# Encoder layer on one core: a factor spread at once over all partitions with its by-token values sent through DRAM, transposes issued in one row, a second norm in four steps, and final results multiplied from PSUM

## The chip, the cores and the metric

The kernel runs on 1 core of one Trainium2 chip. The metric is the device time of one execution in microseconds (us); the time of a kernel is the median of its runs. Engines are named as in the profile: PE is TensorE (matmuls and transposes; PEld is its weight load), DVE is VectorE, ACT is ScalarE, POOL is GpSimd, SP is SyncE, which here only issues DMAs. PSUM is the memory that PE writes, SBUF the memory that all engines share, DRAM the memory off the core.

## The reference, cut to what matters

One layer of a hybrid encoder on 512 tokens with 2048 channels, float32, and a final norm:

```python
rms(x, g) = x * rsqrt(mean(x*x, channels) + EPS) * g

xn   = rms(x, attn_norm_g)
u_val, u_gate, q, k, v = split(xn @ w_in)             # 5 x 1024 columns
y_conv = silu(layer_norm(depthwise_conv31(u_val * sigmoid(u_gate))))
y_na   = neighbourhood_attention(q, k, v, rpb)        # 16 heads, window 8 x 16
x = x + concat(rms(y_conv, conv_out_g), rms(y_na, na_out_g)) @ w_out
xn = rms(x, ffn_norm_g)
gate, val = split(depthwise_conv3(xn @ w_up))         # 2 x 5632 columns
x = x + (silu(gate) * val) @ w_down
return rms(x, final_norm_g)
```

Each RMS norm needs one factor per token, rsqrt(mean + EPS).

## The kernel before, in words

Activations lie transposed: 128 channels on the partitions, the 512 tokens along the free axis, 16 such tiles for 2048 channels. Every operand of a matmul is split into a rounded high part and a low remainder, and a product is three matmuls (`mm3`, L128): high x high, low x high, high x low. Weights arrive in units of 128x1024 (`raw_unit`, L110), ACT makes the high part (L117) and DVE the low part (L121), `AHEAD` = 3 units before PE uses them.

The work is written down as a stream of matmul groups: input projection (`project`, `project_v`; order in `ORDER`, L52), output projection in two halves (`out_half`, L612: first the convolution's half `ma`, then the attention's half `mb`), the up-projection (seven products per pair of blocks, L782 on), the down-projection, and a last stage. Smaller stages are Python generators: `tick` (L141) resumes one of them after each unit of weights, so that their instructions stand in the program behind that unit's last matmul. A scheduler then fixes the order of each engine's queue by its own estimates; `pin` keeps an instruction in program order. On the chip each engine runs its queue in order and waits on semaphores.

Stages that the change touches:

- **First norm** (`stats1` L317, `factor_and_tokens` L225). The squares of the 16 input tiles are summed into `acc1`. Four matmuls with one column each (L231) sum it over the partitions, which gives the factors with tokens on the partitions, 128x4; ACT and DVE take the root there (`root`, L185). That tile, `rtok`, is what the value projection is scaled by when it leaves PSUM (L371, L374). For all other uses the factor must stand on every partition along the tokens: DVE multiplies an identity by the values (L236, L240) and two matmuls with ones spread it (L245); ACT copies it to SBUF (L247) as `rstd1`. The gate of the convolution group (L399) is the first to read `rstd1`.
- **Other norms** (`spread`, L191, called by `factor`). ACT and DVE split the sum of squares into two parts (L195, L196), two matmuls with a 128x128 block of ones (L200) sum over the partitions and spread the sum at once, into the PSUM bank with the tag "po"; ACT takes the root (L204) and three DVE instructions refine it (L205 to L207).
- **Attention.** For each of 8 pairs of heads: `scores` (L501) fills four banks, `softmax` (L517) works on them in the order 2, 3, 0, 1, and some ticks later `turn` (L529) transposes the four tiles with 16 PE transposes (L537) and copies them to SBUF with ACT (L542). Banks 0 and 1 are the two halves of one PSUM tile, `wide`; 2 and 3 are tiles of their own. The tile `ts[n]` is transposed and copied before the next n.
- **Norm of the attention's output** (`norm_b`, L624). After its factor `rna`, DVE scales the 8 tiles (L627), and ACT and DVE split each (L170, L171) into the operands `mb`. It yields once, after the fifth tile. Beside it runs the convolution's half of the output projection, whose banks (tag "mm", three of them) `read_a` empties with DVE (L637, L638).
- **End** (L1005 on). Tokens 0 to 383 leave transposed, as eight pairs of channel tiles; the last 128 tokens are computed the other way round (tokens on the partitions, L1055 to L1068) in four banks `pt`, g = 0 to 3, and leave last (L1091). The factor `rstd3` for the first 384 tokens comes from `spread` after the first bank. `finish` (L1007) multiplies each tile by its gain and by the factor: for pairs 1, 4 and 7 ACT applies the gain (L1014) and POOL multiplies (L1015); for the other five DVE does both in one instruction (L1017). Pairs 0, 2, 3, 5 and 6 are sent in halves (L1019), pairs 1, 4 and 7 whole (L1021). For the last tokens ACT squares each bank and sums it (L1071), DVE multiplies three banks by the gains (L1077), adds the sums (L1073, L1074, L1079), and after a short chain on DVE and ACT (L1080 to L1083) the four results are scaled (L1086, L1088, L1090) and sent.

Of the kernel before, what the change touches and what calls it, by code (L numbers as in the profile page):

```python
# [10 lines left out]
F32 = mybir.dt.float32  # L11
F32R = mybir.dt.float32r
AF = mybir.ActivationFunctionType
ALU = mybir.AluOpType
AX = mybir.AxisListType

P = 128
D = 2048
S = 512
# [9 lines left out]
EPS = 1e-6  # L29
# [3 lines left out]
NP_ = HEADS // 2  # L33
# [33 lines left out]
def layer(ctx: ExitStack, tc: tile.TileContext, xT, xG, xw, w_a, w_in, w_v, w_out, w_up, w_down, par, tab, g3, out, last_out):  # L67
    nc = tc.nc
# [3 lines left out]
    sm = ctx.enter_context(tc.tile_pool(name="sm", bufs=2))  # L72
    dram = ctx.enter_context(tc.tile_pool(name="dram", bufs=1, space=bass.MemoryType.DRAM))
    psm = ctx.enter_context(tc.tile_pool(name="psm", bufs=3, space=bass.MemoryType.PSUM))
    psa = ctx.enter_context(tc.tile_pool(name="psa", bufs=1, space=bass.MemoryType.PSUM))
# [9 lines left out]
    def t2(name, dt=F32):  # L85
        return tp.tile([P, S], dt, tag="t2k", name=name)
# [5 lines left out]
    pin = tc.keep_in_program_order  # L92
# [11 lines left out]
    ones_r = consts.tile([P, P], F32R, name="ones")  # L104
    ones = ones_r.bitcast(F32)
    nc.vector.memset(ones, 1.0)
    ident = consts.tile([P, P], F32, name="ident")
# [74 lines left out]
    eps = consts.tile([P, 1], F32, name="eps")  # L182
    nc.vector.memset(eps, EPS)

    def root(r, y, v):  # L185
        nc.scalar.activation(r, v, AF.Abs_reciprocal_sqrt)
        nc.vector.scalar_tensor_tensor(y, r, -0.5, r, op0=ALU.mult, op1=ALU.mult)
        nc.vector.tensor_mul(y, y, v)
        nc.vector.scalar_tensor_tensor(y, y, 1.5, r, op0=ALU.add, op1=ALU.mult)

    def spread(acc, to, n, name, bank, hold=False):  # L191

        m = to.stop - to.start
        h, l = (t2("n" + c, F32R)[:, :m] for c in "hl")
        nc.scalar.activation(h, acc[:, to], AF.Copy)  # L195
        nc.vector.tensor_sub(l, acc[:, to], h.bitcast(F32))  # L196
        yield
        ps = bank()[:, :m]
        for i, x in enumerate((h, l)):
            x = nc.tensor.matmul(ps, ones_r, x, start=i == 0, stop=i == 1)  # L200
            if hold:
                pin(x)
        r, q = t2(name)[:, :m], t2("q")[:, :m]
        nc.scalar.activation(r, ps, AF.Abs_reciprocal_sqrt, scale=1.0 / n, bias=eps)  # L204
        nc.vector.scalar_tensor_tensor(q, r, -0.5 / n, r, op0=ALU.mult, op1=ALU.mult)  # L205
        nc.vector.scalar_tensor_tensor(q, ps, n * EPS, q, op0=ALU.add, op1=ALU.mult)
        nc.vector.scalar_tensor_tensor(r, q, 1.5, r, op0=ALU.add, op1=ALU.mult)  # L207
        return r

    def stat_bank(free=False):  # L210
        if free:
            return psa.tile([P, 2, S], F32, tag="sc", name="st")[:, 0]
        return psa.tile([P, S], F32, tag="po", name="st")

    def factor(acc, n, name, rest=1, free=False):
        steps = spread(acc, slice(0, S), n, name, lambda: stat_bank(free))
        next(steps)
        for _ in range(rest):
            yield
        try:  # L220
            next(steps)
        except StopIteration as e:
            return e.value

    def factor_and_tokens(acc, n, name, by_token):  # L225

        m = S // P
        ps = stat_bank()[:, :m]
        v, r, y = (sm.tile([P, m], F32, tag="rs" + c, name="rs" + c) for c in "vry")
        for i in range(m):  # L230
            nc.tensor.matmul(ps[:, i:i + 1], acc[:, i * P:(i + 1) * P], ones[:, 0:1], start=True, stop=True)  # L231
        nc.vector.tensor_scalar(v, ps, 1.0 / n, EPS, op0=ALU.mult, op1=ALU.add)
        root(r, y, v)
        by_token.append(y)
        ds = [t2("dg", F32R) for _ in range(2)]
        nc.vector.tensor_mul(ds[0].rearrange("p (i k) -> p i k", k=P), ident.unsqueeze(1).broadcast_to([P, m, P]),  # L236
                             y.unsqueeze(2).broadcast_to([P, m, P]))
        for i in range(m):
            o = slice(i * P, (i + 1) * P)
            nc.vector.scalar_tensor_tensor(ds[1][:, o], ident, y[:, i:i + 1], ds[0][:, o].bitcast(F32),  # L240
                                           op0=ALU.mult, op1=ALU.subtract)
        yield
        ps = stat_bank()
        for i, dg in enumerate(ds):
            nc.tensor.matmul(ps, ones_r, dg, start=i == 0, stop=i == 1)  # L245
        res = t2(name)
        nc.scalar.activation(res, ps, AF.Copy)  # L247
        return res

    xs, x1 = [], []  # L250
    acc1 = t2("acc1")
# [11 lines left out]
    ps = psa.tile([P, 2, S], F32, tag="sc", name="idle")  # L263
# [3 lines left out]
    for k in range(KD):  # L267
        if k < CH:
            raw = t4([P, U * P], "raw")
            n = S + 2 * P + (0 if k else KD)  # L270
# [46 lines left out]
    def stats1():  # L317
        yield
        for k in range(CH, KD):
            with tc.issue_after(made[0][3].ins):  # L320
                sum_sq(acc1, x1[k], False)
            if k % 4 == 3:
                yield
        for _ in range(STAT_AT):
            yield
        rstd.append((yield from factor_and_tokens(acc1, D, "rstd1", rtok)))

    steps.append(stats1())

# [198 lines left out]

    def turn(ts):  # L529
        pts, first = {}, True  # L530
        for n in (2, 3, 0, 1):
            if n == 0:
                wide = psa.tile([P, 2, 4, P], F32, tag="sc", name="trp")
            ps = wide[:, n] if n < 2 else psa.tile([P, 4, P], F32, tag="tr", name="trp", bufs=2)
            for i in range(2):
                for ch in range(2):
                    m = nc.tensor.transpose(ps[:, 2 * i + ch, :], ts[n][:, i, ch * P:(ch + 1) * P], ident)  # L537
                    if not first:
                        pin(m)
                    first = False  # L540
            pts[n] = t2("pt").rearrange("p (c k) -> p c k", c=4)
            nc.scalar.activation(pts[n], ps, AF.Copy)  # L542
        turned.append(pts)
        return pts
# [79 lines left out]
    def norm_b():  # L624
        r = yield from factor(acc_na, NA, "rna")
        for i in range(NP_):
            nc.vector.tensor_mul(aos[i], aos[i], r)  # L627
            mb.append(split(aos[i], pc("nag", i), "mb"))
            if i == NP_ // 2:
                yield  # L630

    def read_a(d, ps):
# [374 lines left out]
    def finish(pair, r, apart=False, split=False):  # L1007

        o = t4([P, 2, LT], "fin")
        for i in range(2):  # L1010
            d = 2 * pair + i
            x, g = x2[d][:, fm], pc("g3", d)
            if apart:
                nc.scalar.activation(x, x, AF.Copy, scale=g)  # L1014
                nc.gpsimd.tensor_mul(o[:, i], x, r)  # L1015
            else:
                nc.vector.scalar_tensor_tensor(o[:, i], x, g, r, op0=ALU.mult, op1=ALU.mult)  # L1017
            if split:
                nc.sync.dma_start(out[pair][:, i], o[:, i])  # L1019
        if not split:  # L1020
            nc.sync.dma_start(out[pair], o)  # L1021
# [9 lines left out]
                pin(nc.scalar.activation(idle, eps, AF.Abs_reciprocal_sqrt))  # L1031
        sum_sq(acc[:, fm], x2[d][:, fm], d == 0, to=fm)

    rows = spread(acc, fm, D, "rstd3", stat_bank, hold=True)
    next(rows)
    wide = psa.tile([P, 2, S], F32, tag="sc", name="pt")
    banks = [psa.tile([P, S], F32, tag="tr", name="pt", bufs=2) if g % 2 else wide[:, g // 2] for g in range(CH)]
# [5 lines left out]
    def along(g, k):  # L1043
        if (g, k) == (1, 0):
            try:
                next(rows)
            except StopIteration as e:
                rb.append(e.value)
        for at in pairs[:2 if rb else 0]:
            pairs.remove(at)  # L1050
            finish(at, rb[0], at % 3 == 1, at % 3 != 1)

    for g, ps in enumerate(banks):
        for i in range(CH):
            m = nc.tensor.matmul(ps[:, i * P:(i + 1) * P], x2[g * CH + i][:, tm], ident, start=i == 0, stop=False,  # L1055
                                 is_transpose=True)
            if g > 1 and i == 0:
                pin(m)
        for k in range(n):
            (hh, hl), (dh, dl) = hs[k], ws[g * CH + k]  # L1060
            i = nc.tensor.matmul(ps, hh[:, tm], dh, start=False, stop=False)
            if (g, k) == (1, 0):
                pin(i)
                along(g, k)
            i = nc.tensor.matmul(ps, hl[:, tm], dh, start=False, stop=False)
            if (g, k) == (1, 0):
                pin(i)
            nc.tensor.matmul(ps, hh[:, tm], dl, start=False, stop=k == n - 1)  # L1068
            if (g, k) != (1, 0):
                along(g, k)  # L1070
        nc.scalar.activation(t2("sq"), ps, AF.Square, accum_out=sums[:, g:g + 1])  # L1071
        if g == CH - 2:
            nc.vector.tensor_reduce(v, sums[:, :CH - 1], axis=AX.X, op=ALU.add)  # L1073
            nc.vector.tensor_scalar(v, v, 1.0 / D, EPS, op0=ALU.mult, op1=ALU.add)  # L1074
        xg.append(t2("xg"))
        if g < CH - 1:
            nc.vector.tensor_mul(xg[g], ps, gains[g])  # L1077
# [91 lines left out]
```

## Time and profile before

| what | before |
|---|---|
| median of 3 runs | 2032.06 us (2030.57 to 2032.34) |
| profiled execution, its own time | 2031.56 us |
| span in its trace | 2029.8 us |
| granted TensorE clock | 0.998 |
| busy: PE, DVE, ACT, POOL | 99%, 82%, 52%, 8% |
| last matmul starts | 2017.90 us |
| DMA volume | 284.25 MB, mean 140 GB/s |

Times in a timeline row are the start in us from the span's beginning, the time until the row's last instruction ended, the engine, the line of the kernel, the operation, output<-inputs by the program's names, shapes, and the count of merged instructions; in square brackets stands the idle time of the engine ahead of the row and the instruction that ended it. Matmuls are pipelined: a 128x512 matmul has a row of 0.39 us, but the next one starts 0.23 us after it. A row of waits is: who waited, for whom, us in total, times, longest.

### The profile page before, as it was taken

The page shows a single profiled execution, that of the slowest core. Times are in us where ns is not written, and L with a number is a line of the kernel's source. Part 1 is how long each engine was busy: PE and PEld are TensorE (multiplying, and loading weights), DVE is VectorE, ACT ScalarE, POOL GpSimd, SP SyncE. Part 2 cuts the span into 40 slices and gives each one's busy share as a digit, 9 for nine tenths or more (in the row PEclk, how much of TensorE's full clock was granted, in tenths as well). Part 3 has the DMA queues.
Part 4 walks back from the last instruction along what each step waited for, and adds up shares of the span by engine and source line. Part 5 has one row for each costly group of instructions (what it writes and reads, how often), then busy time and mean ns, then how long its engine had stood idle before and what let it go on. Part 6 is the DMA issues. An engine that isn't in the chain of part 4 may idle for free.

```text
span 2029.8 us, 28055 instructions
## 1 busy us (share of the span) xinstructions
PE 2008.3 (99%) x10518; PEld 1715.8 (85%) x10518; DVE 1672.3 (82%) x2269; ACT 1052.8 (52%) x1688; POOL 170.5 (8%) x199
## 2 busy tenths in 40 slices
PE   9999999999999999999999999999999999999997
PEld 7888888888778998888888888888888888888887
DVE  7986888987577899888888888788888888889876
ACT  6323334476346655555555555555555555555563
POOL 0000000000001101111111111111111111110111
PEclk9999999999999999999999999999999999999999
DMA  7232323336338765566565565555566565555583
GB/s 256 83 104 91 115 88 106 110 126 214 99 109 221 188 178 145 125 146 145 125 145 145 134 136 146 135 135 145 125 145 146 125 145 146 135 136 135 135 219 113
DMA packets 98935, 284.25 MB, mean 140 GB/s; under 512 B 10992, under 2 KB 12272, under 8 KB 98800
## 3 DMA queue, kind: packets, MB, share of 16 engines
q1 hardware_dynamic: 72144, 231.07, 36.7%
q0 software_dynamic: 26656, 51.39, 17.0%
q8 instruction: 83, 1.36, 0.3%
q14 instruction: 52, 0.43, 0.1%
HBM read 227.89 MB, written 54.53 MB: 139 GB/s over the span
## 4 chain that ended last, share of the span: by engine, by line
PE 97%; DVE 1%; ACT 1%; DMA 0%; issue 0%; ACTq 0%; DVEq 0%
PE pu L791 26%; PE pu L797 14%; PE pd L136 8%; PE pd L131 8%; PE pd L135 8%; PE pj L131 6%; PE pj L135 6%; PE pj L136 6%; PE po L131 3%; PE po L135 3%; PE po L136 3%; PE pv L361 1%; PE pv L360 1%; PE pv L362 1%; PE po L553 1%; PE pu L135 1%
## 5 line engine op out<-in xcount | busy, mean ns | idle before, releaser
L117 ACT ACTIVATE whi<-raw 128x1024 fp32r<-128x1024 f32 x364 | 384.4, 1058 | 492.5 <-PE pj L135 125.4
L121 DVE TENSOR_TENSOR wlo<-raw,whi 128x1024 fp32r<-128x1024 f32 x364 | 444.7, 1223 | 207.7 <-ACT whi L117 199.1
L791 PE MATMUL pu<-xc,whi 128*128 128x512 f32 x2352 | 580.0, 391 | 0.0
L791 PEld LDWEIGHTS pu<-xc,whi 128*128 128x128 f32 x2352 | 433.5, 188 | 83.0
L797 PEld LDWEIGHTS pu<-xc,wlo 128*128 128x128 f32 x2352 | 306.8, 191 | 14.6
L797 PE MATMUL pu<-xc,wlo 128*128 128x256 f32 x2352 | 311.3, 283 | 0.0
L136 PE MATMUL pd<-hh,wlo 128*128 128x512 f32 x640 | 250.3, 391 | 0.0
L131 PE MATMUL pd<-hh,whi 128*128 128x512 f32 x640 | 249.6, 390 | 0.0
L135 PE MATMUL pd<-hl,whi 128*128 128x512 f32 x640 | 249.1, 389 | 0.0
L945 POOL DMA_DIRECT2D x2d<-pdc x160 | 139.3, 872 | 1097.4 <-ACT pdc L944 869.6
L131 PE MATMUL pj<-xh,whi 128*128 128x512 f32 x512 | 198.4, 392 | 0.3 <-ACT g L297 0.3
L135 PE MATMUL pj<-xl,whi 128*128 128x512 f32 x512 | 198.3, 390 | 0.0
L136 PE MATMUL pj<-xh,wlo 128*128 128x512 f32 x512 | 198.2, 390 | 0.0
L823 ACT ACTIVATE pl<-pu 128x256 f32<-128x256 f32 x294 | 109.7, 381 | 149.5 <-PE pu L791 142.6
L117 ACT ACTIVATE whi<-ws 128x1024 fp32r<-128x1024 f32 x132 | 139.8, 1059 | 73.9 <-PE pu L791 54.0
L416 DVE SCALAR_TENSOR_TENSOR y<-ch,prm,y 128x500 f32<-128x500 f32 (+14 forms) x240 | 173.6, 742 | 4.3
L121 DVE TENSOR_TENSOR wlo<-ws,whi 128x1024 fp32r<-128x1024 f32 x132 | 161.3, 1222 | 14.5 <-ACT whi L117 14.5
L136 PEld LDWEIGHTS pd<-hh,wlo 128*128 128x128 f32 x640 | 120.1, 188 | 28.4 <-DVE wlo L121 3.3
L135 PEld LDWEIGHTS pd<-hl,whi 128*128 128x128 f32 x640 | 120.2, 188 | 24.9 <-DVE hl L930 0.3
L131 PEld LDWEIGHTS pd<-hh,whi 128*128 128x128 f32 x640 | 120.4, 188 | 22.7
L944 ACT ACTIVATE pdc<-pd 128x512 f32<-128x512 f32 x160 | 93.8, 588 | 79.0 <-PE pd L136 65.9
L131 PEld LDWEIGHTS pj<-xh,whi 128*128 128x128 f32 x512 | 96.0, 188 | 21.4 <-ACT g L297 0.5
(237 smaller groups left out, 2730.3 us busy)
## 6 DMA issues: line engine op xcount, KB each, us to landing
raw<-in_w_up SPq DMA_DIRECT2D x176, 512.0 KB, 3.8
raw<-in_w_down SPq DMA_DIRECT2D x88, 512.0 KB, 3.9
x2d<-pdc POOLq DMA_DIRECT2D x160, 256.0 KB, 4.9
raw<-in_w_in SPq DMA_DIRECT2D x60, 512.0 KB, 3.8
raw<-in_w_out SPq DMA_DIRECT2D x32, 512.0 KB, 3.8
raw<-in_w_v SPq DMA_DIRECT2D x16, 512.0 KB, 3.8
tab<-in_tab SPq DMA_DIRECT2D x32, 256.0 KB, 5.2
x<-in_xT SPq DMA_DIRECT2D x16, 256.0 KB, 6.0
```

Source lines behind the costliest of these rows:

```text
L117: i = nc.scalar.activation(hi[:, :n], raw[:, :n], AF.Copy)
L121: j = nc.vector.tensor_sub(lo[:, :n], raw[:, :n], hi[:, :n].bitcast(F32))
L131: m = nc.tensor.matmul(ps, hi[:, a], mh, start=start, stop=False)
L135: nc.tensor.matmul(ps, hi[:, a], ml, start=False, stop=False)
L136: return nc.tensor.matmul(ps, lo[:, a], mh, start=False, stop=stop)
L360: nc.tensor.matmul(ps, xh, wh[:, f], start=kk == 0, stop=False)
L416: nc.vector.scalar_tensor_tensor(y[:, a:b], h[:, a + j - PAD:b + j - PAD], prm[:, o + j:o + j + 1], y[:, a:b], op0=ALU.mult, op1=ALU.add)
L791: i = nc.tensor.matmul(ps, w[0][:, k * P:(k + 1) * P], comb[c][k], start=k == 0, stop=stop and k == ks[-1])
L797: i = nc.tensor.matmul(ps[:, H:], w[1][:, k * P:(k + 1) * P], comb[c][k][:, :H], start=False, stop=stop and k == U - 1)
L823: nc.scalar.activation(to, ps, AF.Copy)
L944: nc.scalar.activation(t, ps, AF.Copy)
L945: nc.gpsimd.dma_start(xd[d], t, accum_op=ALU.add)
```

## The change

1. The first norm uses `spread` through `factor` like the others: the sum of squares is split, and two matmuls sum and spread it at once. The by-token values are got by writing one row of the result, 512 values, to DRAM and reading it back as 128x4, both DMAs on POOL's queue. `root` and `factor_and_tokens` go.
2. In `spread`, the second matmul is pinned in every use.
3. `turn` takes all four banks first, issues the 16 transposes in one row, and then the four copies.
4. `norm_b` yields after every second tile.
5. At the end, `spread` leaves the refined factor in its PSUM bank and ACT copies it to SBUF. DVE's multiplications read it from PSUM, POOL's from SBUF.
6. Only pairs 0 and 2 are sent in halves. The spread sum's two matmuls stand ahead of the first product of bank 1 instead of behind it.

```diff
-    def root(r, y, v):
...
-    def spread(acc, to, n, name, bank, hold=False):
+    def spread(acc, to, n, name, bank, hold=False, both=False):
...
             x = nc.tensor.matmul(ps, ones_r, x, start=i == 0, stop=i == 1)
-            if hold:
+            if i or hold:
                 pin(x)
...
+        if both:
+            nc.vector.scalar_tensor_tensor(ps, q, 1.5, r, op0=ALU.add, op1=ALU.mult)
+            nc.scalar.activation(r, ps, AF.Copy)
+            return ps, r
         nc.vector.scalar_tensor_tensor(r, q, 1.5, r, op0=ALU.add, op1=ALU.mult)
         return r
...
-    def factor_and_tokens(acc, n, name, by_token):
...
+    def by_token(r):
+        row, y = dram.tile([1, S], F32, name="row"), sm.tile([P, S // P], F32, tag="rtok", name="rtok", bufs=1)
+        nc.gpsimd.dma_start(row, r[:1])
+        nc.gpsimd.dma_start(y, row.rearrange("o (t p) -> p (o t)", p=P))
+        return y
...
-        rstd.append((yield from factor_and_tokens(acc1, D, "rstd1", rtok)))
+        rstd.append((yield from factor(acc1, D, "rstd1")))
+        rtok.append(by_token(rstd[0]))
...
     def turn(ts):
         pts, first = {}, True
-        for n in (2, 3, 0, 1):
-            if n == 0:
-                wide = psa.tile([P, 2, 4, P], F32, tag="sc", name="trp")
-            ps = wide[:, n] if n < 2 else psa.tile([P, 4, P], F32, tag="tr", name="trp", bufs=2)
+        banks = [psa.tile([P, 4, P], F32, tag="tr", name="trp", bufs=2) for _ in range(2)]
+        wide = psa.tile([P, 2, 4, P], F32, tag="sc", name="trp")
+        banks += [wide[:, 0], wide[:, 1]]
+        order = (2, 3, 0, 1)
+        for n, ps in zip(order, banks):
             for i in range(2):
                 for ch in range(2):
                     m = nc.tensor.transpose(ps[:, 2 * i + ch, :], ts[n][:, i, ch * P:(ch + 1) * P], ident)
...
+        for n, ps in zip(order, banks):
             pts[n] = t2("pt").rearrange("p (c k) -> p c k", c=4)
             nc.scalar.activation(pts[n], ps, AF.Copy)
...
             mb.append(split(aos[i], pc("nag", i), "mb"))
-            if i == NP_ // 2:
+            if i % 2:
                 yield
...
-    rows = spread(acc, fm, D, "rstd3", stat_bank, hold=True)
+    rows = spread(acc, fm, D, "rstd3", stat_bank, hold=True, both=True)
...
-                rb.append(e.value)
+                rb.extend(e.value)
...
-            finish(at, rb[0], at % 3 == 1, at % 3 != 1)
+            finish(at, rb[at % 3 == 1], at % 3 == 1, at in (0, 2))
...
             (hh, hl), (dh, dl) = hs[k], ws[g * CH + k]
+            if (g, k) == (1, 0):
+                along(g, k)
             i = nc.tensor.matmul(ps, hh[:, tm], dh, start=False, stop=False)
             if (g, k) == (1, 0):
                 pin(i)
-                along(g, k)
-            i = nc.tensor.matmul(ps, hl[:, tm], dh, start=False, stop=False)
-            if (g, k) == (1, 0):
-                pin(i)
+            nc.tensor.matmul(ps, hl[:, tm], dh, start=False, stop=False)
```

More of the change, by code (lines that the diff above doesn't have):

```diff
@@ L183, in layer @@
     nc.vector.memset(eps, EPS)
-    def root(r, y, v):
[L186 to L189, printed above, removed]
-    def spread(acc, to, n, name, bank, hold=False):
+    def spread(acc, to, n, name, bank, hold=False, both=False):
         m = to.stop - to.start
@@ L223, in factor @@
             return e.value
-    def factor_and_tokens(acc, n, name, by_token):
[L227 to L248, printed above, removed]
+    def by_token(r):
[3 more added lines that the diff above has]
+        return y
     xs, x1 = [], []
```

## The prediction

> **What bounds the kernel now.** I read the page first, then who waited on PE, then busy time on both sides of the last matmul.
>
> ```profile
> span 2029.8 us, 28055 instructions
> ...
> PE 2008.3 (99%) x10518; PEld 1715.8 (85%) x10518; DVE 1672.3 (82%) x2269; ACT 1052.8 (52%) x1688; POOL 170.5 (8%) x199
> ...
> PE 97%; DVE 1%; ACT 1%; DMA 0%; issue 0%; ACTq 0%; DVEq 0%
> ```
>
> ```profile
> PE trp L537 <- ACT pt L542: 6.2, 6, 1.1
> PE po L131 <- DVE oa L637: 2.4, 2, 2.0
> ```
>
> ```profile
> 0.00:2018.30 2018.30, 2008.28 (x10518) 1715.82 (x10518) 1665.74 (x2255) 1050.62 (x1683) 169.05 (x198) 1.00 0.54 139
> 2018.30:2029.80 11.50, 0.00 (x0) 0.00 (x0) 6.57 (x15) 2.22 (x5) 1.41 (x2) 0.63 0.71 262
> ```
>
> PE is 97% of the chain that ended last. Until its last matmul ends at 2018.3 it idles 10.0 us (2018.30 less 2008.28), and 8.6 of these stand in the two rows of waits: transposes behind ACT's copies, and the output projection behind DVE's `oa`. After 2018.3 PE does nothing for 11.5 us. So there are three kinds of gain: a PE stall that goes, PE work that goes, and a shorter tail. A stall that goes counts in full, since no other engine bounds PE elsewhere. The granted clock is 1.00 throughout, so the clock is no term.
>
> **Part 1: the 16 transposes of `turn`, six times.**
>
> ```profile
> 254.34 1.47 PE L537 MATMUL trp<-ident,tab 128*128 128x128 f32 x12
> 255.27 1.55 ACT L542 ACTIVATE pt<-trp 128x512 f32<-128x512 f32 x3
> 256.88 0.66 PE L537 MATMUL trp<-ident,tab 128*128 128x128 f32 x4 [1.07 <-ACT pt L542]
> 257.29 0.49 PE L131 MATMUL pj<-xh,whi 128*128 128x512 f32 x1
> ...
> 405.20 1.47 PE L537 MATMUL trp<-ident,tab 128*128 128x128 f32 x12
> 406.43 0.48 PE L131 MATMUL pj<-xh,whi 128*128 128x512 f32 x1
> ```
>
> The last four transposes (n = 1) wait until ACT has copied n = 0: both write one PSUM tile, `wide`, and the copy of its first half stands before them in the program. At 405.20 twelve transposes cost 1.23 us up to the next start, and four cost 0.41 (256.88 to 257.29): 1.64 in all. The stalled turn takes 2.95 (254.34 to 257.29), 1.31 more, which is 0.24 more than its idle column, as row ends run past the next start. In the other two of the eight turns matmuls already fill the gap. Six stalls: 6.2 + 6 x 0.24 = **7.6 us**. With all transposes ahead of the copies this wait cannot occur. Next late would be the softmax of n = 1 on DVE, the last of its kind:
>
> ```profile
> 435.98 0.69 DVE L527 TENSOR_TENSOR tab<-tab,su 128x512 f32<-128x512 f32 x1
> ```
>
> ```profile
> 439.08 1.47 PE L537 MATMUL trp<-ident,tab 128*128 128x128 f32 x12
> ```
>
> Here, at its tightest, it is done 2.4 us ahead of the turn, and the built order of the changed program keeps it there. The copies move by less than 2 us; `values` reads them a whole weight unit later (24 matmuls of 0.23 us, 5.4). Bounds: nothing if the tile is still waited for, 7.9 with the slower restarts.
>
> **Part 2: `norm_b` in four steps.**
>
> ```profile
> 573.37 0.39 PE L136 MATMUL po<-mah,wlo 128*128 128x512 f32 x1
> 575.75 0.50 PE L131 MATMUL po<-mah,whi 128*128 128x512 f32 x1 [1.99 <-DVE oa L637]
> 581.90 0.47 PE L131 MATMUL po<-mah,whi 128*128 128x512 f32 x1 [0.42 <-DVE oa L637]
> ```
>
> ```profile
> 567.47 1.90 DVE L627 TENSOR_TENSOR ao<-ao,rna 128x512 f32<-128x512 f32 x3
> 575.00 0.69 DVE L637 TENSOR_TENSOR oa<-po,ra 128x512 f32<-128x512 f32 x1
> ```
>
> From 567.47 DVE works through the norm, and the bank that PE wants at about 573.6 is emptied at 575.00. In the built order this `oa` now follows four L627 and two L171, not seven and five: 6 x about 0.62 us from 567.47 gives 571.2. The second `oa` comes about 4 us later, ahead of PE's need at 579. The first stall is 573.37 to 575.75 less one step of 0.23: 2.15; the second at least its 0.42. I take **2.6 us** (0 if a new order stalls elsewhere). The price is that the last `mbl` is made later, by my count near 584.6; PE reads it 21 matmuls (4.8 us) into the second half, which then begins at 584.6.
>
> **Part 3: the first norm.**
>
> ```profile
> 40.85 0.68 DVE L180 TENSOR_TENSOR acc<-acc,sq 128x512 f32<-128x512 f32 x1
> 41.82 0.95 PE L231 MATMUL st<-ones,acc 128*128 128x1 f32 x8
> 42.62 0.49 PE L136 MATMUL pj<-xh,wlo 128*128 128x512 f32 x1
> 47.00 0.69 DVE L399 TENSOR_TENSOR gate<-pj,rstd 128x512 f32<-128x512 f32 x1 [1.23 <-ACT rstd L247]
> 53.35 0.69 DVE L404 TENSOR_TENSOR ch<-pj,gate 128x512 f32<-128x512 f32 x1
> 55.07 0.39 PE L360 MATMUL pv<-whi,xh 128*128 128x512 f32 x1
> ...
> 559.45 0.69 DVE L196 TENSOR_TENSOR nl<-accna,nh 128x512 fp32r<-128x512 f32 x1 [0.70 <-ACT nh L195]
> 565.29 0.69 DVE L205 SCALAR_TENSOR_TENSOR q<-rna 128x512 f32<-128x512 f32 x1 [0.78 <-ACT rna L204]
> ```
>
> The one-column matmuls go: 41.82 to 42.62, **0.8 us** of PE. The two spreading matmuls stay two. New latency: `acc1` is done at 41.5; ACT's split 0.70 and DVE's 0.69 end at 42.9, before PE comes to the pinned pair at about 44.2, so nothing queues behind it. Then ACT's root (about 0.7) and three DVE steps of 0.69 put `rstd1` at 47.7, 0.7 later than now. What waits for it: the gates, and through them the banks of the first value projection. The tightest is now freed at 54.04 (53.35 + 0.69) and used at 55.07; in the built order its first matmul stands 25 places into that projection instead of 17, so about 1 us of room stays. DVE gives up 0.16 x 4, 0.69 and 1.15 us and takes up four times 0.69: nothing.
>
> ```profile
> 92.90 0.69 ACT L371 ACTIVATE vg<-pv,rsy 128x512 f32<-128x512 f32 x1 [2.56 <-PE pv L362]
> ```
>
> ```profile
> x2d<-pdc POOLq DMA_DIRECT2D x160, 256.0 KB, 4.9
> ```
>
> The by-token values are first read at 92.90, less the 0.8 gained: 44 us after 47.7. No row shows a DMA of four-byte pieces; the nearest, POOL's accumulating write, lands in 4.9 us, so write and read back are about 10, nothing else being in POOL's queue until 598 us. Cost nothing; for the other end see the last rival.
>
> **Part 4: the end.**
>
> ```profile
> L206 DVE SCALAR_TENSOR_TENSOR q<-st,q 128x384 f32<-128x384 f32 x1 | 0.6, 558 | 0.0
> ```
>
> ```profile
> L1017 DVE SCALAR_TENSOR_TENSOR fin<-x,prm,rstd x10: 605/1350/1374, 2011.8 to 2021.1; 128x384 f32<-128x384 f32 x10
> ```
>
> ```profile
> 2011.80 9.91 DVE L1017 SCALAR_TENSOR_TENSOR fin<-x,prm,rstd 128x384 f32<-128x384 f32 x10
> 2011.91 7.80 POOL L1015 TENSOR_TENSOR fin<-x,rstd 128x384 f32<-128x384 f32 x6 [37.23 <-DVE rstd L207]
> ...
> 2018.82 0.19 ACT L1071 ACTIVATION_READ_ACCUMULATOR sq<-pt 128x1 f32 x1
> 2021.63 0.68 DVE L1077 TENSOR_TENSOR xg<-pt,g3b 128x512 f32<-128x512 f32 x1
> 2023.14 0.16 DVE L1079 SCALAR_TENSOR_TENSOR rsv<-rsl,rsv 128x1 f32<-128x1 f32 x1
> 2024.56 1.80 SPq L1091 DMA_DIRECT2D out_N<-xg x4
> ```
>
> DVE's ten multiplications run from 2011.80 to 2021.7, and only then come L1077 and the closing chain, though ACT's last sum is there at 2019.0. A multiplication takes 605 ns at best and 1350 in the median; six slow ones lie beside POOL's six (7.80 us, 1.30 each), and once POOL is done they are short again. So DVE takes turns with POOL. Both read two operands from SBUF; now DVE reads one from PSUM. The trace has no such instruction beside POOL's; the nearest row by operands is L206 (one input from PSUM, 558 ns), the bounds are 0.6 and 1.30 a step. I take 0.6, because what the two share must be a way into SBUF.
>
> The Trainium skill, page "SBUF — State Buffer", section "Who interferes with whom", says that a DVE instruction with two SBUF inputs contends with a GpSimd one that reads SBUF, and one with at most one SBUF input does not. The slow 1350 ns agrees with its first half; no run so far shows the second, by which the sum is the one below.
>
> DVE starts 0.23 earlier, as the sum's matmuls stand one matmul ahead: 2011.57 + 6.0 = 2017.6; two L1077 and two tiny ones (1.4) end at 2019.0. ACT's sum ends at 2019.0 too, so L1079 runs at 2019.1 instead of 2023.14: **4.0 us**. What is late next: POOL begins after ACT's added copy (0.6) at 2012.3, ends by 2020.1 at 1.30 a step, and SP sends pair 7 by 2020.5, just when the first last result is ready (2024.56 less 4.0). Three fewer DMAs on SP then cost or gain nothing, since SP waits for POOL.
>
> **Sum.** 7.6 + 2.6 + 0.8 + 4.0 = 15.0 us. The profiled execution took 2031.56 (span 2029.8 and 1.76 around it): 2016.6. The median, 2032.06, lies 0.5 higher, which I leave to the range.
>
> **Rivals.**
>
> *DVE and POOL still alternate* (2020.4). Then L1017 stays at 9.9 us and only the 0.23 of the earlier start is left of the tail's 4.0. For it: the output and the gain pointer are still in SBUF. Against: no row. 0.08.
>
> *A new wait in the reordered middle* (2017.5 to 2019.5).
>
> ```profile
> 478.77 1.28 ACT L204 ACT_TABLE_LOAD   x1
> ...
> 480.06 0.69 ACT L204 ACTIVATE ra<-st,eps 128x512 f32<-128x512 f32 x1
> ```
>
> The sum for `ra` now stands 24 matmuls (5.4 us) later, and the attention's values reuse its bank 24 matmuls after it. Before that, ACT loads its table (1.28), takes the root (0.69), and DVE runs three instructions of 0.69, one a key tile in between: 4.0 us in a row, with a weight copy ahead. About 1 us of room; each us missed is PE's, and losing part 2 as well gives 2019.2. 0.06.
>
> *The change doesn't do what it says in `turn`* (2024.2): the four still wait on the tile as a whole, 7.6 less. The built order has no copy between them. 0.02.
>
> *Slower: the way through DRAM.* One mechanism, at 92 us: ACT cannot empty the value banks before the by-token tile is back, and PE's next projection needs them. It decides from a round trip of 44 us; at 59 all 15 us are spent, and from 63 the kernel is slower by over 0.2%. That needs 0.12 us for each of 512 values in a row. Against: 10 us by the nearest row. 0.02.
>
> The same page, section "A bandwidth-pool intuition that's wrong (but worth ruling out)", has a DMA of GpSimd's queue stretched from 620 to 3100 ns by DVE. Five times 10 us would be 50, an estimate, and the time 6 us above the forecast; no trace here shows it.
>
> **How the numbers follow.** Forecast 2016.6 with 0.82; its own range is 2014.5 to 2018, from the spread of the runs shown (2030.57 to 2032.34) and 0.3 more or less in each part. The range to 2020.8 takes in the first two rivals. A measurement tells about 0.2%, 4 us, from no change: faster 0.96, same 0.02, slower 0.02.
>
> **What would show it.** Right: no row PE trp <- ACT pt, none PE po <- DVE oa; the last matmul 11 us earlier; L1017's successor at about 600 ns throughout beside POOL at 1.3 us; 7.5 us from the last matmul to the end. Wrong: multiplications of 1.3 us there, a new row of waits on PE over 1 us near 50, 92, 486 or 585, or POOL holding back the last results.

## The result and the profile after

The changed kernel takes **2016.64 us** (median of 6 runs, 2016.15 to 2017.5) where the kernel before took 2031.91 (median of 6 runs beside them). The ratio is 0.9925, 95% interval 0.9913 to 0.9938: 15 us, as forecast (2016.6). The profiled execution took 2016.15. The total fits better than its terms do: the sum contains two errors that nearly cancel. That shows only when the two traces are cut at the same places.

The page of the changed kernel, first its span, busy times and shares of the chain that ended last:

```profile
span 2014.4 us, 28027 instructions
...
PE 2004.4 (100%) x10510; PEld 1715.7 (85%) x10510; DVE 1667.9 (83%) x2264; ACT 1054.7 (52%) x1689; POOL 169.4 (8%) x201
...
PE 99%; DMA 0%; ACT 0%; DVE 0%; ACTq 0%; issue 0%; DVEq 0%
```

What PE waited for, in the changed kernel (us in total, times, longest):

```profile
PE idle L244 <- POOL warm L103: 1.1, 1, 1.1
```

Both rows on which the prediction built, `trp` behind ACT and `po` behind DVE, are gone. What is left is the start of the kernel. Busy times on both sides of the last matmul's end (length, then busy time and count of PE, PEld, DVE, ACT and POOL, granted clock, DMA share, GB/s):

```profile
0.00:2005.65 2005.65, 2004.42 (x10510) 1715.71 (x10510) 1665.57 (x2257) 1052.50 (x1684) 169.36 (x201) 1.00 0.55 140
2005.65:2014.40 8.75, 0.00 (x0) 0.00 (x0) 2.35 (x8) 2.22 (x5) 0.00 (x0) 0.62 0.76 292
```

PE now idles 1.2 us in all up to its last matmul's end (2005.65 less 2004.42), and 1.1 of them are the row above. The last matmul starts at 2005.25, 12.65 us earlier, where the prediction had 11. From its end to the end of the span it is 8.75 us instead of 11.5, and the prediction had 7.5. To see what each part gave, I took the start of the same instruction in both traces at seven places and subtracted. The places are DVE's L121 at 39 us, before anything changed has an effect; the first `pv` matmul; the first transpose of a turn; the first matmul behind the last turn; the first matmul that reads `mbh`; the first behind the second norm's sum (near 676); and the last matmul.

| from, to | before | changed | gain | predicted | with that part undone |
|---|---|---|---|---|---|
| start to L121 | 39.71 | 39.02 | 0.7 | none | 38.80 to 39.63 in kernels with the same code |
| to first `pv` (first norm) | 11.51 | 10.30 | 1.2 | 0.8 | 11.48 |
| to first turn | 203.12 | 203.13 | 0.0 | 0 | |
| to behind the last turn | 289.29 | 281.41 | 7.9 | 7.6 | 289.20 |
| to `mbh` (`norm_b`) | 43.84 | 40.84 | 3.0 | 2.6 | 43.82 |
| to behind the second norm's sum | 101.89 | 101.89 | 0.0 | 0 | |
| to the last matmul | 1328.54 | 1328.66 | -0.1 | 0 | |
| to the end of the span (tail) | 11.90 | 9.15 | 2.75 | 4.0 | 12.44 (the operand alone) |

The gains sum to 15.4, the difference of the spans. PE gave 12.0 instead of 11.0, and the start 0.7 that is not the change's. The tail gave 1.25 less than predicted. Rows of the changed kernel behind the table, first PE in a turn and at the first norm's sum (start, length, engine, line, operands):

```profile
43.40 0.39 PE L194 MATMUL st<-nh,ones 128*128 128x512 f32 x1
43.63 0.39 PE L194 MATMUL st<-nl,ones 128*128 128x512 f32 x1
43.86 0.40 PE L131 MATMUL pj<-xh,whi 128*128 128x512 f32 x1
...
252.45 1.91 PE L518 MATMUL trp<-ident,tab 128*128 128x128 f32 x16
254.11 0.48 PE L131 MATMUL pj<-xh,whi 128*128 128x512 f32 x1
...
574.70 0.39 PE L131 MATMUL po<-mbh,whi 128*128 128x512 f32 x1
...
2005.25 0.39 PE L1049 MATMUL pt<-dl,hh 128*128 128x512 f32 x1
```

Sixteen transposes run through in 1.66 us (252.45 to 254.11), where the stalled turn took 2.95. DVE in the changed kernel's `norm_b` and ahead of the gates:

```profile
46.97 0.69 DVE L379 TENSOR_TENSOR gate<-pj,rstd 128x512 f32<-128x512 f32 x1
...
565.69 0.69 DVE L619 TENSOR_TENSOR oa<-po,ra 128x512 f32<-128x512 f32 x1
...
569.96 0.69 DVE L619 TENSOR_TENSOR oa<-po,ra 128x512 f32<-128x512 f32 x1
...
574.16 0.75 DVE L171 SCALAR_TENSOR_TENSOR mbl<-ao,prm,mbh 128x512 fp32r<-128x512 f32 x1
```

The two `oa` come 4.3 us apart and early, the last `mbl` is finished by 574.9, and PE starts on the second half at 574.70 without a gap. The by-token values on POOL's queue, and their first reader on ACT:

```profile
47.26 0.70 POOL L225 DMA_DIRECT2D row<-rstd  x1 [45.69 <-DVE rstd L205]
49.98 0.82 POOL L226 DMA_DIRECT2D rtok<-row  x1 [2.02 <-DMA row<-rstd]
```

```profile
91.00 0.69 ACT L351 ACTIVATE vg<-pv,rtok 128x512 f32<-128x512 f32 x1 [2.56 <-PE pv L342]
```

The landings are in the table of DMAs below. Now the end. DVE's and POOL's multiplications as groups (ns minimum, median, maximum; first and last start), then DVE, POOL and SP in order of time:

```profile
L999 DVE SCALAR_TENSOR_TENSOR fin<-x,prm,st x10: 607/610/616, 1999.5 to 2004.2; 128x384 f32<-128x384 f32 x10
```

```profile
L997 POOL TENSOR_TENSOR fin<-x,rstd x6: 1012/1016/1027, 1999.5 to 2004.4; 128x384 f32<-128x384 f32 x6
```

```profile
1998.31 0.57 DVE L202 SCALAR_TENSOR_TENSOR st<-q,rstd 128x384 f32<-128x384 f32 x1
1999.49 2.72 DVE L999 SCALAR_TENSOR_TENSOR fin<-x,prm,st 128x384 f32<-128x384 f32 x5 [0.62 <-ACT rstd L203]
...
2006.40 0.16 DVE L1060 SCALAR_TENSOR_TENSOR rsv<-rsl,rsv 128x1 f32<-128x1 f32 x1 [0.24 <-ACT sq L1052]
```

```profile
2000.14 0.86 SPq L1001 DMA_DIRECT2D out_T<-fin  x2
...
2002.99 3.93 SPq L1003 DMA_DIRECT2D out_T<-fin  x5
2007.81 2.54 SPq L1072 DMA_DIRECT2D out_N<-xg  x4
```

All ten multiplications take 610 ns beside POOL. L1060, the old L1079, stood 5.24 us behind the last matmul's start before (2023.14 against 2017.90) and now stands 1.15 behind it: 4.1 us earlier. The first `out_N` issue follows it by 1.41 us, as before. But from that issue to the end of the span it is 6.6 us (2007.81 to 2014.40) instead of 5.24. The four issues take 2.54 us instead of 1.80. The table of DMAs (KB each, median us from issue to landing) and the DMA engines in slices of 2 us:

```profile
out_T<-fin SPq DMA_DIRECT2D x6, 384.0 KB, 4.4
out_N<-xg SPq DMA_DIRECT2D x4, 256.0 KB, 3.4
...
row<-rstd POOLq DMA_DIRECT2D x1, 2.0 KB, 2.4
rtok<-row POOLq DMA_DIRECT2D x1, 2.0 KB, 2.6
```

```profile
2002.40:2004.40 2.00, 2.00 (x13) 1.69 (x12) 2.00 (x5) 0.69 (x2) 2.00 (x3) 1.00 1.01 376
...
2006.40:2008.40 2.00, 0.00 (x0) 0.00 (x0) 1.79 (x6) 1.30 (x3) 0.00 (x0) 0.84 1.01 398
...
2010.40:2012.20 1.80, 0.00 (x0) 0.00 (x0) 0.00 (x0) 0.00 (x0) 0.00 (x0) 0.50 0.99 377
```

The kernel before, in two slices of its end:

```profile
2017.80:2019.80 2.00, 0.49 (x3) 0.06 (x1) 2.00 (x2) 0.69 (x2) 1.91 (x2) 1.00 0.31 112
...
2023.80:2025.80 2.00, 0.00 (x0) 0.00 (x0) 1.32 (x4) 1.33 (x2) 0.00 (x0) 0.50 0.49 186
```

The last two columns carry the finding. Before, the DMA engines had holes, and the last results (the slice from 2023.8) met idle engines. Now the engines are full from 2002.4 to 2012.2, at 376 to 398 GB/s, and the last results queue behind `out_T`.

### The profile page after: what moved, and what is told of

Its sections match the earlier page's. It is cut to its first block, busy times and chain, and to the rows that moved or that the text cites. A ratio compares the mean times of both kernels' runs of the same rounds, so it can differ in the third digit from the quotient of the medians.

```text
span 2014.4 us, 28027 instructions
## 1 busy us (share of the span) xinstructions
PE 2004.4 (100%) x10510; PEld 1715.7 (85%) x10510; DVE 1667.9 (83%) x2264; ACT 1054.7 (52%) x1689; POOL 169.4 (8%) x201
## 4 chain that ended last, share of the span: by engine, by line
PE 99%; DMA 0%; ACT 0%; DVE 0%; ACTq 0%; issue 0%; DVEq 0%
PE pu L773 27%; PE pu L779 14%; PE pd L136 8%; PE pd L131 8%; PE pd L135 8%; PE pj L131 6%; PE pj L135 6%; PE pj L136 6%; PE po L131 3%; PE po L135 3%; PE po L136 3%; PE pv L342 1%; PE pv L341 1%; PE pv L340 1%; PE po L535 1%; PE trp L518 1%
## 5 line engine op out<-in xcount | busy, mean ns | idle before, releaser
L121 DVE TENSOR_TENSOR wlo<-raw,whi 128x1024 fp32r<-128x1024 f32 x364 | 444.5, 1222 | 208.5 <-ACT whi L117 198.0
L396 DVE SCALAR_TENSOR_TENSOR y<-ch,prm,y 128x501 f32<-128x501 f32 (+14 forms) x240 | 173.5, 740 | 4.4
L121 DVE TENSOR_TENSOR wlo<-ws,whi 128x1024 fp32r<-128x1024 f32 x132 | 161.2, 1221 | 14.8 <-ACT whi L117 14.8
```

Source lines behind the costliest of these rows:

```text
L121: j = nc.vector.tensor_sub(lo[:, :n], raw[:, :n], hi[:, :n].bitcast(F32))
L396: nc.vector.scalar_tensor_tensor(y[:, a:b], h[:, a + j - PAD:b + j - PAD], prm[:, o + j:o + j + 1], y[:, a:b], op0=ALU.mult, op1=ALU.add)
```

## The experiments

**The theory:** the parts on PE add up, each by its own stall; at the end the PSUM operand frees DVE, and then the bytes to be written bind. **The rivals:** the tail is held by SP's issues, or by the chain behind the last matmul; the multiplications are fast for another reason; the 0.7 us at the start belongs to the change.

Tails are from the last matmul's start to the end of the span, each from one profiled execution; spans are given to 0.1 us, so a tail is good to about 0.05. Each kernel is the changed one with the edit shown, unless said otherwise.

**1. The old `turn`.**

```
-        banks = [psa.tile([P, 4, P], F32, tag="tr", name="trp", bufs=2) for _ in range(2)]
-        wide = psa.tile([P, 2, 4, P], F32, tag="sc", name="trp")
...
-        for n, ps in zip(order, banks):
+        for n in (2, 3, 0, 1):
+            if n == 0:
+                wide = psa.tile([P, 2, 4, P], F32, tag="sc", name="trp")
+            ps = wide[:, n] if n < 2 else psa.tile([P, 4, P], F32, tag="tr", name="trp", bufs=2)
...
-        for n, ps in zip(order, banks):
```

> The changed kernel with `turn` as it was before: PSUM tile `wide` is written in part after ACT's copy of its first half. Theory (the stall of the last four transposes is worth what the trace says): a row PE trp <- ACT pt of about 6 us in 6 stalls comes back, the last matmul starts 7.6 to 7.9 us later than in the changed kernel (2005.25), the tail stays 9.15 us (start of the last matmul to the end of the span); time about 2024.4. Rival (the stall is made up elsewhere, because PE also waits for something else there): under 4 us.

2024.25 us. What PE waited for:

```profile
PE trp L517 <- ACT pt L522: 6.1, 6, 1.1
```

The stage of the turns is 289.20 us again instead of 281.41, and every other stage and the tail (9.19) stay. So this part is worth 7.8 us.

**2. The old `norm_b`.**

```
-            if i % 2:
+            if i == NP_ // 2:
                 yield
```

> The changed kernel with `norm_b` in two steps as before. Theory: the row PE po <- DVE oa of about 2.4 us in 2 stalls comes back and the last matmul starts 2.6 to 3.0 us later; tail unchanged at 9.15; time about 2019.4. Rival (the 3.0 us seen near 575 belong to the later start of the sum of `ra` or another moved instruction, not to these steps): no stall row, under 1 us.

2020.3 us. What PE waited for:

```profile
PE po L131 <- DVE oa L619: 2.4, 2, 2.0
...
PE st L194 <- DVE nl L190: 0.6, 1, 0.6
```

The stage is 43.82 instead of 40.84: 3.0 us, and the tail is 9.16. The second row is new and costs PE another 1.0 us in this execution, at 679 us, at the second norm's sum. There the change only pins the second matmul, which starts right behind the first in the kernel before too. It came up in other runs too; see below.

**3. The old first norm.**

```
-        rstd.append((yield from factor(acc1, D, "rstd1")))
-        rtok.append(by_token(rstd[0]))
+        rstd.append((yield from factor_and_tokens(acc1, D, "rstd1", rtok)))
```

> The changed kernel with the first norm's factor made as before (one-column matmuls, root, diagonal spread) and without the way through DRAM. Theory: 8 one-column matmuls return at about 42, PE's first `pv` matmul stands 0.8 to 1.2 us later, counted from DVE's first L121 behind the start-up; tail unchanged; time about 2017.5. The 0.69 us by which the changed kernel's start-up was earlier before any changed instruction runs is expected to be a difference between executions, so DVE's instruction at 39.0 us may stand anywhere between 39.0 and 39.7. Rival (the start-up is shorter because of the change): it stands at 39.7 again and the time is 1.9 us longer.

2017.27 us. L121 stands at 39.11, and the first `pv` 11.48 behind it, as in the kernel before. PE in this kernel:

```profile
41.22 0.95 PE L235 MATMUL st<-ones,acc 128*128 128x1 f32 x8
42.02 0.49 PE L136 MATMUL pj<-xh,wlo 128*128 128x512 f32 x1
42.35 0.40 PE L131 MATMUL pj<-xh,whi 128*128 128x512 f32 x1
...
44.90 0.39 PE L135 MATMUL pj<-xl,whi 128*128 128x512 f32 x1
45.22 0.50 PE L249 MATMUL st<-dg,ones 128*128 128x512 f32 x1
45.55 0.40 PE L136 MATMUL pj<-xh,wlo 128*128 128x512 f32 x1
```

The eight small matmuls take 0.80 us up to the next start. The matmul behind them takes 0.33 up to its successor instead of 0.23, the second spreading matmul starts 0.32 behind its predecessor, and its own step is 0.33: three times 0.1, most of the 0.4 that the prediction lacked. L121 at 39.11 with the old code, and at 39.34 in experiment 5, settles the start: it was a difference between executions. Against the expectation the tail is 8.78, not 9.15.

**4. DVE multiplies by the copy in SBUF.**

```
-            finish(at, rb[at % 3 == 1], at % 3 == 1, at in (0, 2))
+            finish(at, rb[1], at % 3 == 1, at in (0, 2))
```

> The changed kernel, but DVE's ten multiplications of the end read the factor's copy in SBUF, as POOL does, in place of PSUM; all else, the whole pairs too, as changed. Theory (two SBUF operands make DVE and POOL alternate): multiplications of 605 ns alone and about 1350 ns beside POOL, POOL about 1300 ns, DVE's series 9.9 us long instead of 5.9, L1060 5.6 us after the start of the last matmul instead of 1.15; tail about 12.2 instead of 9.15 us; time about 2019.7. Rival (the multiplications are faster for another reason, such as fewer DMA issues): 610 ns, tail 9.15.

2020.78 us, tail 12.44. The two groups:

```profile
L999 DVE SCALAR_TENSOR_TENSOR fin<-x,prm,rstd x10: 604/1348/1376, 2000.6 to 2009.9; 128x384 f32<-128x384 f32 x10
```

```profile
L997 POOL TENSOR_TENSOR fin<-x,rstd x6: 1306/1318/1447, 2000.7 to 2007.2; 128x384 f32<-128x384 f32 x6
```

One operand's place makes 1348 ns of 610, and 1318 of POOL's 1016. The Trainium skill, page "SBUF — State Buffer", section "Who interferes with whom", has a DVE instruction with at most one SBUF input, outside the 2-port perf modes, not contend with GpSimd; this pair of kernels agrees, if the gain's column, which comes from SBUF in both, is not counted.

**5. The kernel before with the new end alone** (the edits of `spread`, `finish`'s call and the sum's place).

> The kernel before with only the end changed: factor in PSUM for DVE and a copy for POOL, whole pairs but for 0 and 2, and the sum's two matmuls one matmul earlier. Theory: the last matmul starts where it did before (2017.9, with the start-up's spread of 0.7), the tail is 9.15 us instead of 11.90; 2.75 us faster than before, 2028.8. What the prediction held: 4.0 faster. Rival (the tail is short only together with the other parts): under 2 us.

2028.66 us beside 2032.12, ratio 0.9984, interval 0.9975 to 0.9994. The tail is 8.77: 3.1 us less than before. So the end's gain needs no other part, and it isn't 4.0 here either. In this execution PE took 1.2 us longer than before between the last turn and the second norm's sum; 0.3 of it is the wait near 676. The other 0.9 stand behind the old first stall of `norm_b`, in which PE idled 1.99 us until 575.39. The engines from 576.3 to 579.4 us (columns as above):

```profile
576.30:579.40 3.10, 3.10 (x9) 2.35 (x9) 3.10 (x5) 0.40 (x1) 0.00 (x0) 0.51 0.04 7
```

The granted clock was 0.51 there, and the matmuls start 0.43 us apart instead of 0.23. Eight such steps cost 1.6 us; 0.7 comes back, as the old second stall of 0.42 and its slower restart then do not occur. The kernel before and kernel 2 have the same stall of 1.99 us and kept a clock of 1.00 behind it. So a stall can cost more in single executions than its own row says; why it did in this one isn't shown.

**6. Three DMAs fewer** (pairs 5, 6 and 7 of `out_T` are computed and not written).

```
-        if not split:
+        if not split and pair < 5:
             nc.sync.dma_start(out[pair], o)
```

> The changed kernel without the three DMAs that send pairs 5, 6 and 7 of `out_T` (1.18 of 4.19 MB are not written; every multiplication is still done). Theory (at the end the DMA engines are full, and the last results queue behind `out_T`): the last four DMAs issue in about 1.8 us and land in about 2.5 us, as in the kernel before, and the tail is 2.56 + 5.24 = 7.8 us, 1.35 less than 9.15. Rival (the last DMAs are slow by themselves, by SP's issues or by when ACT and DVE finish their tiles): the tail stays within 0.3 of 9.15 and each issue takes about 0.6 us.

2015.47 us, tail 7.65. SP in order of time, and the table of DMAs:

```profile
2008.51 1.80 SPq L1072 DMA_DIRECT2D out_N<-xg  x4
```

```profile
out_N<-xg SPq DMA_DIRECT2D x4, 256.0 KB, 2.5
```

Issues and landings are back at the values of the kernel before (1.80 and 2.5), with every computation in place. The bytes ahead of the last results are what makes them late.

**7. Halves as before** (`at % 3 != 1` for `at in (0, 2)`).

> The changed kernel with pairs 0, 2, 3, 5 and 6 sent in halves, as before (three more DMAs on SP). Theory (bytes, not issues, bind the end): the tail stays within 0.3 us of 9.15. Rival (SP's issues bind): three more issues of 0.4 us, the tail 0.6 to 1.2 us longer.

2017.21 us, tail 9.02. Three more DMAs on SP cost nothing: issues don't bind. (The time holds a wait of 1.4 us near 676.)

**8. The last results on two queues.**

```
-        nc.sync.dma_start(last_out[:, g * S:(g + 1) * S], xg[g])
+        (nc.scalar if g % 2 else nc.sync).dma_start(last_out[:, g * S:(g + 1) * S], xg[g])
```

> The changed kernel with the second and fourth of the last results sent by ACT instead of SP. Theory (the DMA engines are full): the issues overlap, but the last landing and the end stay within 0.3 us. Rival (SP's 2.54 us of four issues in a row set the end): up to 1.2 us less.

2016.95 us, tail 9.23. SP's two issues and ACT's two overlap, and each lands later:

```profile
out_N<-xg SPq DMA_DIRECT2D x2, 256.0 KB, 3.9
out_N<-xg ACTq DMA_DIRECT2D x2, 256.0 KB, 4.2
```

The Trainium skill, page "DMA: Bandwidth & Descriptors", section "Issuing engines are not separate DMA queues", says that the issuing engine gives a DMA no engines of its own; this run agrees.

**9. Another order of pairs.** `pairs = [0, 2, 1, 3, 5, 4, 6, 7]`, so that SP doesn't stand behind POOL's pair 1.

> The changed kernel with the pairs of the end in the order 0, 2, 1, 3, 5, 4, 6, 7, so that SP does not wait for POOL's pair 1 (issued at 2001.58) ahead of DVE's pair 2. Theory (writes bind from the first byte on): the slice from 2002.0 to 2002.5, where the DMA share is 0.36, fills up, and the end comes about 0.3 us earlier. Rival (what binds is the chain behind the last matmul): no change, within 0.1.

2016.3 us, tail 8.80. The hole at the start of the writing is gone, and the end comes 0.35 us sooner. The theory that bytes bind from the first one on asked for 0.3. It is one execution against one: kernels with the same end have tails of 9.05 to 9.19, and two (3 and 5) lie 0.4 lower for a reason that stays open (experiments 11 and 12 look for it).

**10. DVE free of ACT's copy, with that order of pairs.**

```
+            p2 = psm.tile([P, S], F32, tag="mm", name="r2")[:, :m]
+            nc.scalar.activation(p2, r, AF.Copy)
+            nc.vector.scalar_tensor_tensor(p2, q, 1.5, p2, op0=ALU.add, op1=ALU.mult)
+            b = t2("q")[:, :m]
+            nc.scalar.activation(b, q, AF.Copy, bias=1.5)
+            nc.gpsimd.tensor_mul(r, b, r)
-            nc.vector.scalar_tensor_tensor(ps, q, 1.5, r, op0=ALU.add, op1=ALU.mult)
-            nc.scalar.activation(r, ps, AF.Copy)
...
```

> The order of pairs 0, 2, 1, 3, 5, 4, 6, 7, and DVE does not wait for ACT's copy of the factor: ACT copies the raw root into another PSUM bank early, DVE finishes the factor there in place and multiplies at once, and ACT and POOL make POOL's copy of the factor from SBUF by themselves. Theory (writes bind from the first byte on): DVE's first multiplication starts 0.6 us sooner after the factor (0.62 of idle gone), the first DMA too, and the tail is 0.6 to 0.9 us shorter than 9.15: about 8.4, time 2015.9. Rival (what binds is the chain behind the last matmul): no change; if POOL's later start (by about 0.3 us) holds SP up, 0.3 longer.

2015.77 us (2015.53 to 2017.0), ratio to the kernel before 0.9922, interval 0.9910 to 0.9935. SP's first and last issues, and the last matmul:

```profile
2001.04 1.91 SPq L1005 DMA_DIRECT2D out_T<-fin  x4
...
2009.25 1.94 SPq L1076 DMA_DIRECT2D out_N<-xg  x4
```

```profile
2006.68 0.39 PE L1053 MATMUL pt<-dl,hh 128*128 128x512 f32 x1
```

The first DMA goes out 5.64 us ahead of the last matmul instead of 5.11, and the tail is 8.52, 0.63 less: 0.35 by the order and 0.28 by the earlier start. The expectation gave the start more, 0.6. The start came 0.5 earlier, but about 0.2 us of that went into a new hole while SP waited for POOL:

```profile
2003.68:2004.68 1.00, 1.00 (x8) 0.88 (x7) 1.00 (x3) 0.69 (x2) 1.00 (x2) 1.00 0.80 300
```

In the whole time this can't be told from the changed kernel, whose interval is 0.9913 to 0.9938. In the profiled execution, the slowest of this kernel's five at 2017.0, the last matmul starts 1.4 us later than in the changed one, 0.6 of it by the start and 0.95 by the wait near 676.

**11. The by-token DMAs sent by SP**, in the changed kernel, **and 12. in kernel 10.** (`nc.gpsimd.dma_start` in `by_token` becomes `nc.sync.dma_start`.)

> The changed kernel with the two small DMAs of the by-token values sent by SP instead of POOL. At 47 to 52 us SP has nothing else to send (its next issue stands at 56.57), so the stages up to the last matmul should not move. The tail was 9.15 to 9.23 us in three kernels with the small DMAs on POOL's queue and 8.77 to 8.78 in the two without them; the last bytes move 0.4 us longer in the former. Theory A (those two DMAs change how later transfers spread over the DMA engines): tail about 8.8. Theory B (that difference has another cause, or the SP's two also shift it): 9.15 or another value; then it stays open.

> The kernel with the pairs reordered and DVE free of ACT's copy, and the by-token values' DMAs sent by SP. Theory A of the run beside it: a tail of about 8.2 us (8.52 less up to 0.4). Theory B: 8.5. The time, with the spread of start-up (0.9 us) and of the wait near 676 (1.4 us), 2014.8 to 2016.5, where the changed kernel has 2016.6.

2016.87 us with a tail of 9.05, and 2016.47 with 8.41. So the sender of those DMAs isn't why the tail is 0.4 shorter in the two kernels without them (3 and 5). That stays open. Kernel 12 has the shortest tail of those that write everything, and its time is not apart from the changed kernel's.

**The wait near 676 us.** Eight of these twelve profiles (2 to 7, 10 and 12) held PE up at the second norm's sum, by 0.3 to 1.5 us; those of the kernel before, of the changed one and of the other four did not. In the changed kernel and in kernel 7, DVE:

```profile
673.10 0.69 DVE L684 TENSOR_TENSOR acc<-acc,sq 128x512 f32<-128x512 f32 x1
```

```profile
674.93 0.69 DVE L684 TENSOR_TENSOR acc<-acc,sq 128x512 f32<-128x512 f32 x1 [1.96 <-DMA sq<-sq]
```

The second norm's squares are summed in DRAM, and the load of the sum comes when it comes. PE needs the result 3 us later, so a late one reaches it. Kernel 5, which has the first three parts as before, waits there too, by 0.3 us. I take it for the spread in when that load lands. This isn't shown: no run changed it alone, only two of the fourteen kernels have the first three parts as before, and the six waits above 0.8 us are all in others.

## Why the prediction was right, step by step

- **The turns: right.** The six stalls were worth 7.8 to 7.9 us against 7.6. The idle column plus the slower restart was the way to price them; the restart is a little dearer than 0.24.
- **`norm_b`: right, too small.** 3.0 against 2.6. I took a step off the first stall and counted the second by its idle column alone. The two rows sum to 2.4, so the restarts cost 0.6. The late `mbl` did no harm.
- **The first norm: right, too small.** 1.2 against 0.8, by the small steps in experiment 3. The way through DRAM took 5.3 us from issue to landing (47.26 to 49.98 plus 2.6) where I put 10, and is done 38 us before its reader. The page "SBUF — State Buffer" of the Trainium skill, section "A bandwidth-pool intuition that's wrong (but worth ruling out)", would have allowed DMAs of GpSimd's queue to be stretched; these two landed in 2.4 and 2.6 us, the load sent by SP (experiment 11) in 2.1, and no run here shows it.
- **The tail: the mechanism right, the size wrong (2.75 against 4.0).** That L1060 moves up by 4 us came true (4.1), and at 610 ns as taken. The first of the last DMAs went out 2.56 us behind the last matmul's start, where the prediction had 2.66. What failed is the step "what is late next". I weighed SP's queue and POOL, with POOL at 1.30 us a step until 2020.1, "just when the first last result is ready". POOL was faster (1.016 us a step) and done 0.2 us behind the last matmul's start instead of 2.2, because it no longer shared either, and SP was idle when the last results came. The next bound was the one that I didn't count: `out_T` and `out_N` are 8 x 384 and 4 x 256 KB, 4.19 MB, and at 390 GB/s that is 10.8 us of full DMA engines from the first byte on. So the wait of the last results behind `out_T` was put at nothing and took 1.35 us (6.59 from the first issue to the end, against 5.24). The numbers were in the profile before. The holes in its writing were what the faster DVE would fill.
- **The added copy** was put at 0.6 us for POOL alone. DVE waited for it as well (0.62 us of idle ahead of the first L999), though both only read the bank. The prediction had DVE start 0.23 us sooner before the last matmul; it started 0.34 later. L1060 did not notice: DVE's multiplications start 0.53 us apart, so ten took 5.34 us where the prediction put 6.0, and L1060 waited for ACT's sum alone. But the writing began later by it; that costs about 0.3 us (experiment 10).
- **The rivals.** DVE and POOL do not alternate, and experiment 4 shows what that would have cost: 2020.78, where the rival's price was 2020.4. In its profiled execution 0.85 us of the time are the wait near 676, so the match is partly luck: its tail is 12.44, where the rival had 11.67 (11.90 less 0.23). No new wait came up in the reordered middle: the stages around 486 and 585 us last as long in every kernel that has these parts as changed. The turn does what it says. The way through DRAM isn't late.

So the total was hit with a tail 1.25 us too short in the sum, PE 1.0 us too long, and a start that happened to be 0.7 us quicker in the profiled execution.

## What to carry to other kernels

When a stall at the end of a kernel goes, add up the bytes that are still to be written and divide by the rate that the trace shows when the DMA engines are full; holes in the DMA row ahead of the last stores are room that a faster engine will use up. If DVE and POOL work side by side on SBUF, look for an operand of DVE that can live in PSUM: both gain. To check a sum of several parts, cut both traces at the same instructions and undo each part by itself; a total that fits can hide errors that cancel.

## What the runs showed of the hardware

- A multiplication of 128x384 on DVE took 610 ns beside POOL with one of its two tensors in PSUM, and 1348 with both in SBUF. POOL's took 1016 and 1318 ns. So when they share, POOL loses too, by 0.3 us each.
- 16 DMA engines wrote results at 376 to 398 GB/s when full. In that state a DMA of 256 KB landed 3.4 us after its issue instead of 2.5, and SP's issue itself grew from 1.80 to 2.54 us for four.
- A store of 2 KB to DRAM and its load back as 128x4 values landed in 2.4 and 2.6 us on POOL's queue; the trace records that load as 16 packets of 128 bytes. On SP's queue the load landed in 2.1 us, as 512 packets of 4 bytes.
- As built, the program does not let DVE and ACT read one PSUM tile at the same time at the end: DVE's first multiplication waited 0.62 us for a copy that only reads.
- Behind a stall of PE of 1.99 us the granted clock was 0.51 from 576.3 to 579.4 us in one execution (kernel 5), and 1.00 in two others with the same stall (the kernel before and kernel 2).
- Kernels whose code is the same up to there reached the same instruction (L121) 38.80 to 39.63 us after the start, in eleven executions.
